# Layer 0 of a two-layer attention kernel: which maxima are turned at a unit's end, and where the totals of the unit before stand

## The chip, the cores and the metric

The kernel runs on one core of one Trainium2 chip. The metric is the device time of one execution in microseconds (us); less is better. Before the change it is 1690.28 us, the median of three runs (1688.93 to 1690.34).

## The reference, cut to what matters

Two attention layers over 1024 latent tokens and 256 context tokens of width 1024. The change touches the softmax attention of layer 0 alone: 16 heads of width 64, four heads share one key/value head. Latent queries see all 1280 keys, context queries only the 256 context keys.

```
def gqa_attend(q, k, v):
    s = jnp.einsum('bqhgd,bkhd->bhgqk', q, k).astype(jnp.float32) * (GQA_HEAD_DIM ** -0.5)
    p = jax.nn.softmax(s, axis=-1).astype(v.dtype)
    return jnp.einsum('bhgqk,bkhd->bqhgd', p, v)

def gqa_mixer(h, hc, p, cos, sin, with_ctx_out):
    ...
    o = sweep_query_blocks(lambda qb: gqa_attend(qb, k_all, v_all), q).reshape(B, S, GQA_WIDTH)
    y = (o * jax.nn.silu(g)) @ p["w_out"]
    ...
        oc = gqa_attend(qc, kc, vc).reshape(B, L, GQA_WIDTH)
        yc = (oc * jax.nn.silu(gc)) @ p["w_out"]
```

## The kernel before, in words

**Units.** Layer 0's attention runs over 20 units, one after the other, numbered here from 0. Sixteen are latent: one head, 1024 queries, ten tiles of 128 keys (`kts` has ten entries). Four are small, for the context queries of the four heads of a group: two key tiles. The small units stand at 4, 9, 18 and 19. The last latent unit, 17, is cut into a part of six key tiles and a part of four (`cut`).

**One unit, in stages.** For each key tile TensorE (PE) makes the scores (`st`, L545), transposed, so that keys lie on partitions and queries along the row. ScalarE (ACT) makes p = exp (L552). After the last tile comes the *unit's end*: PE multiplies the value tiles with all p (`avt`, L600, one pair of matmuls for the two halves of the queries, and since the operands are f32 each is two in the profile: four records per key tile).

**Maxima.** The softmax needs the largest score of each query beforehand. It is found ahead of time: between the score matmuls of one unit PE makes plain score products for later units into a PSUM tile `mx`, and VectorE (DVE) reduces each to a column of `m` (L430 for latent keys, L432 for context keys). One such step is issued for each key tile, 14 steps ahead at the start; a latent unit needs ten, a small one two. So the maxima of a small unit are done soon after those of the unit ahead of it, and all of them are done when unit 16 ends.

**A turn.** The maxima stand as columns and have to become rows. `do_shift` puts a function `turn` on the list `turns`: PE transposes `m` into an `mx` tile (L459), DVE copies the 8x128 result into the SBUF tile `crow` (L461), and two DMAs on SyncE's queue (SP) move it into one row of each half of the tile `shift` (L464). The scores of that unit take the row in as a fourth product (`st<-shift,minus`). `crow` has one buffer, and `mx` has two in PSUM. `run_turns` empties the whole list at each unit's end.

**Totals.** `finish` copies a unit's output out of PSUM and puts a function `total` on the list `totals`. It runs at the end of the next latent unit: PE sums p over partitions into an `mx` tile (L645, weights `twos`), DVE transposes and inverts it (L649, L650), a DMA spreads it (`rrow`, then `rb`), GpSimd (POOL) scales the output (L664, L665) and a DMA stores it in `od` (L669).

**Order at a unit's end.** PE, DVE and ACT take their instructions in the order of the code (`manual_schedule`); for SP and POOL a scheduler orders them. In `run` the end reads: turns, the pairwise sums of the last p tiles on DVE (`pair_sum`, L572), the totals of the unit before, a piece of weight loading for the output projection (`extra`, `parts`, at odd units; it splits f32 weights on ACT, L158, and on DVE or POOL, L137), then the value matmuls (`do_av`). When no maxima are left to compute, the output `avt` is not taken from the score tiles' pool but from the two `mx` buffers (`av_tile`); that is so from unit 16's end on.

Of the kernel before, what the change touches and what calls it, by code (L numbers as in the profile page):

```python
# [11 lines left out]
F32R = mybir.dt.float32r  # L12
# [7 lines left out]
P = 128  # L20
# [9 lines left out]
WIDE = (True, False)  # L30


def raw(ap):
    return ap.bitcast(F32)
# [3 lines left out]
def hybrid_kernel(ctx: ExitStack, tc: tile.TileContext, ins: dict, out: bass.AP):  # L38
# [197 lines left out]
    class Plan:  # L236
# [8 lines left out]
        def run(self):  # L245
            engines = mybir.EngineType
            with tc.manual_schedule(engines={engines.PE, engines.Activation, engines.DVE, engines.Pool, engines.SP}):
                for _, _, fn, args in sorted(self.todo, key=lambda e: e[:2]):
                    fn(*args)
# [60 lines left out]
    class Attention:  # L310
# [134 lines left out]
        def do_shift(self, u):  # L445

            s = self.state[id(u)]
            if u["kind"] == "lat":
                m = self.sm.tile([P, 8], F32, name="m1", tag="m1")
                dve.reduce_max(m, s["m"], axis=AX.X)  # L450
            else:
                m = s["m"][:, :, 0]

            def turn():
                if not WIDE[self.l]:
                    t = self.ps_m.tile([P, 512], F32, name="mx", tag="mx")[:8, :P]
                else:
                    t = self.ps_m.tile([P, 1024], F32, name="mx", tag="mx")[:8, :P]
                pe.transpose(t, m, ident)  # L459
                r = self.sm.tile([8, P], F32R, name="crow", tag="crow", bufs=1)  # L460
                dve.tensor_copy(r, t)  # L461
                if HALVES[self.l]:
                    for n in range(2):
                        sp.dma_start(raw(s["crow"][n]), raw(r[4 * n:4 * n + 4, :]))  # L464
                else:
                    sp.dma_start(raw(s["crow"]), raw(r))

            self.turns.append(turn)

        def start_unit(self):  # L470
            u = self.units[self.started]
# [115 lines left out]
                s["sum"] = t  # L587
            s["total"] = ([s["sum"]] if held else []) + last

        def do_av(self, u, group, ps):  # L590

            s = self.state[id(u)]
            kts = u["kts"]
            if group[0] == kts[0]:
                if not WIDE[self.l]:
                    s["av"] = self.ps_o.tile([P, 512], F32, name="av", tag="av")
                s["v"] = self.load_v(u)
            for kt, p in zip(group, ps):
                for n in range(2):
                    pe.matmul(s["av"][64 * n:64 * n + 64, :], lhsT=s["v"][:, kt, u["vc"]:u["vc"] + 64],  # L600
                              rhs=p[:, n * 512:(n + 1) * 512], start=kt == kts[0], stop=kt == kts[-1])
            if group[-1] == kts[-1]:
                self.finish(u)
# [66 lines left out]

            self.totals.append(total)

        def run_turns(self):
            while self.turns:
                self.turns.pop(0)()

        def run(self, lead, ahead, extra, tail):

            count = lead
            parts = None  # L680
            with tc.manual_schedule(engines={mybir.EngineType.PE, mybir.EngineType.DVE, mybir.EngineType.Activation}):
                for t, u in enumerate(self.units):
                    kts = u["kts"]
                    for v in self.units[t:t + 2]:
                        self.load_v(v)
                    while self.started < min(t + 1 + ahead, len(self.units)):
                        self.start_unit()
                    whole = len(kts) > 4
                    cut = 6 if u is self.last_lat else 0

                    def one_more():
                        nonlocal count
                        count += 1
                        self.maxima(count, t + 1 + ahead)

                    for group in (kts[:cut], kts[cut:]):
                        if not group:
                            continue
                        end = group[-1] == kts[-1]
                        final = t == len(self.units) - 1 and end  # L700
                        p2s = [self.pp.tile([P, 2, 1024], F32, name="p", tag="p", bufs=5) for _ in range(len(group) // 2)]
                        ps = [p2[:, a, :] for p2 in p2s for a in range(2)]

                        late = not whole and t >= len(self.units) - 2
                        n1 = len(ps) - (4 if whole and end else 2 if late else 0)
                        for i, kt in enumerate(group):
                            self.run_deferred(self.step)
                            if HALVES[self.l]:
                                count += 1 if WIDE[self.l] else 2
                                self.scores_by_halves(u, kt, ps[i], self.next_maxima(count, t + 1 + ahead))  # L710
                            else:
                                self.do_scores(u, kt, ps[i], one_more)
                            self.step += 1
                            if i < n1:
                                self.add_up(u, [ps[i]], [])
                        if end and t + 2 < self.started:
                            self.state[id(self.units[t + 2])].pop("rest", lambda: None)()
                        if final:
                            tail()
                        if WIDE[self.l] and group[0] == kts[0]:  # L720
                            self.av_tile(u)
                        self.run_turns()
                        if late or final:
                            self.add_up(u, [], ps[n1:])
                        elif n1 < len(ps):
                            sums = [self.pair_sum(p2) for p2 in p2s[n1 // 2:]]
                            self.add_up(u, *(([], sums) if cut else (sums, [])))
                        if final:
                            self.run_deferred(self.step + 2)
                        gap = 0  # L730
                        while self.totals and (whole or late or final):
                            self.totals.pop(0)(gap)
                            gap += 3
                        if t % 2 and end:
                            if parts:
                                parts()
                            parts = extra.pop(0)() if extra else None
                        self.do_av(u, group, ps)
                        self.step += (2 + len(group)) // 3
                gap = 0  # L740
                while self.totals:
                    self.totals.pop(0)(gap)
                    gap += 3
            self.run_deferred(self.step)
# [522 lines left out]
    def l0_open(at, st):  # L1267
        pool_ = st.enter_context(tc.tile_pool(name="shift0", bufs=1, **right))
        at.minus = pool_.tile([P, 4, P], F32R, name="minus")
        at.shift = pool_.tile([P, 512], F32R, name="shift")  # L1270
        pool.memset(raw(at.shift), 0.0)
        for i in range(4):
            a, b = (ident[:, j:j + 1].broadcast_to([P, P]) for j in (i, 64 + i))
            dve.scalar_tensor_tensor(at.minus[:, i, :], a, -1.0, b, op0=ALU.mult, op1=ALU.subtract)
# [89 lines left out]
    for g, pos in ((0, 4), (1, 9), (3, 18), (2, 19)):  # L1364
        units.insert(pos, ctxu[g])

    at = Attention(0, units, dict(scale=0.125, load=l0_load, scores=l0_scores, maxima=l0_maxima, mparts=1, open=l0_open, gaps=(4, 8, 11), kbufs=2, qbufs=3, vw=256))
    stE = ExitStack()
    with tc.tile_pool(name="wkg0a", bufs=4, **right) as wkg:
# [301 lines left out]
    for p_ in range(8):  # L1671
        for par in range(2):
            h = 2 * p_ + par
            units.append(dict(kind="lat", h=h, pair=p_, par=par, vg=(h // 4, 128 * (h // 2 % 2)), vc=64 * par,
                              kts=list(range(TT))))
    at = Attention(1, units, dict(scale=float(96 ** -0.5), load=l1_load, scores=l1_scores, maxima=l1_maxima, mparts=2, open=l1_open, gaps=(4, 6, 9),
                                  kbufs=3, qbufs=3, vw=128))
# [201 lines left out]
```

## Time and profile before

| what | value |
|---|---|
| median of three runs | 1690.28 us |
| the profiled execution's own time | 1689.1 us |
| its span, first to last instruction | 1687.3 us |
| PE busy | 1646.1 us, 98% of the span |
| DVE busy | 1044.1 us, 62% |
| POOL busy | 949.1 us, 56% |
| ACT busy | 641.2 us, 38% |
| unit 0's end begins (its transpose on PE) | 376.32 us |
| unit 16's end begins | 693.06 us |

Times in a profile's rows count from the first instruction. A row of the timeline has the start, the time to the last end, the engine, the line, the operation and its tiles, the shape, the number of merged instructions and, in brackets, how long the engine was idle before and what ended that. PEclk in a row by stretches is the granted TensorE clock, 1.00 at full speed. PE, busy 98%, is the engine whose idle time counts; for the others idle time counts where PE waits for them.

### The profile page before, as it was taken

Reading aid. Unit: us, or ns where it says so; the run is one execution under the profiler, and the core shown is the slowest. Engines: PE = TensorE matmul, PEld = TensorE weight load, DVE = VectorE, ACT = ScalarE, POOL = GpSimd, SP = SyncE. Lnnn points to the kernel's source line nnn. Section 1 sums busy time; section 2 is a strip of 40 time slices with the busy share of each in tenths; the row PEclk is TensorE's granted clock in tenths of the full one; section 3 lists DMA queues with packets and bytes.
Section 4 is the critical chain, followed back from the end, with each engine's and each line's share of the span. In section 5 each row is a group of like instructions: output and inputs, shape, how many; then the busy total and the mean of one; then the engine's idle time right before and its main releaser. Section 6 shows DMA issues by size and latency. Waiting matters only on the chain. (4 is left out here: it accounts for less than half of the span.)

```text
span 1687.3 us, 27273 instructions
## 1 busy us (share of the span) xinstructions
PE 1646.1 (98%) x10236; PEld 1191.6 (71%) x10236; DVE 1044.1 (62%) x1660; ACT 641.2 (38%) x944; POOL 949.1 (56%) x624
## 2 busy tenths in 40 slices
PE   8999999999999999899989999999999999999998
PEld 5776768875555555458878798886766767667587
DVE  3765553457787887426675657754777777777231
ACT  4642212235444555333234633330534434334310
POOL 2673431128889998742335644450668778777521
PEclk9999999999999999999999999999999999999999
DMA  9557855532342522256424866776565555653351
GB/s 311 176 147 236 268 155 180 160 94 57 99 116 76 138 70 70 55 148 195 141 80 131 238 176 187 227 206 150 126 143 139 132 131 120 134 135 82 121 172 70
DMA packets 221116, 244.21 MB, mean 145 GB/s; under 512 B 23160, under 2 KB 160616, under 8 KB 220984
## 3 DMA queue, kind: packets, MB, share of 16 engines
q1 hardware_dynamic: 220560, 242.36, 51.4%
q8 instruction: 81, 1.33, 0.3%
q14 instruction: 51, 0.42, 0.1%
q10 hardware_dynamic: 424, 0.11, 0.0%
HBM read 168.62 MB, written 73.63 MB: 144 GB/s over the span
## 5 line engine op out<-in xcount | busy, mean ns | idle before, releaser
L552 ACT ACTIVATE p<-st 128x1024 f32<-128x1024 f32 x328 | 336.2, 1027 | 154.1 <-PE st L545 140.8
L586 POOL TENSOR_TENSOR acp<-acp,p 128x1024 f32<-128x1024 f32 x128 | 305.1, 2384 | 7.8
L394 DVE TENSOR_REDUCE m<-mx 128x1 f32<-128x512 f32 x256 | 176.2, 691 | 93.7 <-PE mx L392 88.0
L430 DVE TENSOR_REDUCE m<-mx 128x1 f32<-128x1024 f32 x128 | 150.4, 1220 | 67.2 <-PE mx L421 66.7
L586 POOL TENSOR_TENSOR acp<-p 128x1024 f32<-128x1024 f32 x34 | 81.5, 2399 | 185.2 <-ACT p L552 185.2
L586 POOL TENSOR_TENSOR acp<-acp,acd 128x1024 f32<-128x1024 f32 x60 | 142.4, 2374 | 20.4 <-DVE acd L572 17.2
L600 PE MATMUL avt<-p,v 128*64 128x512 f32 x672 | 151.3, 602 | 1.6 <-DVE crow L461 1.5
L572 DVE TENSOR_REDUCE acd<-p 128x512 f32<-128x1024 f32 x124 | 144.7, 1220 | 7.8 <-ACT p L552 7.8
L600 PE MATMUL av<-p,v 128*64 128x512 f32 x640 | 141.1, 595 | 0.0
L137 POOL TENSOR_TENSOR wb<-wraw,wa 128x512 fp32r<-128x512 f32 (+3 forms) x65 | 85.9, 1337 | 81.8 <-ACT wa L158 80.9
L94 PE MATMUL mm<-wa,hh 128*128 128x512 f32 (+2 forms) x336 | 126.3, 376 | 1.7 <-ACT hh L947 1.7
L545 PE MATMUL st<-QH,KH 64*128 64x512 f32 x320 | 122.4, 407 | 0.6 <-DVE gth L304 0.5
L96 PE MATMUL mm<-wa,hl 128*128 128x512 f32 (+2 forms) x336 | 120.8, 360 | 1.4 <-DVE hl L950 1.4
L95 PE MATMUL mm<-wb,hh 128*128 128x512 f32 (+2 forms) x336 | 120.2, 358 | 0.0
L545 PE MATMUL st<-QH,KL 64*128 64x512 f32 x320 | 117.9, 391 | 0.0
L545 PE MATMUL st<-QL,KH 64*128 64x512 f32 x320 | 117.4, 390 | 0.0
L600 PEld LDWEIGHTS avt<-p,v 128*64 128x64 f32 x672 | 46.6, 138 | 96.6 <-issue 85.9
L94 PE MATMUL y<-wa,oh 128*128 128x512 f32 (+1 forms) x296 | 114.1, 386 | 0.6 <-ACT oh L786 0.6
L96 PE MATMUL y<-wa,ol 128*128 128x512 f32 (+1 forms) x296 | 113.5, 384 | 0.1
L95 PE MATMUL y<-wb,oh 128*128 128x512 f32 (+1 forms) x296 | 113.5, 383 | 0.0
L600 PEld LDWEIGHTS av<-p,v 128*64 128x64 f32 x640 | 44.4, 137 | 88.3 <-issue 87.6
L94 PE MATMUL mm<-hh,wa 128*128 128x512 f32 (+1 forms) x264 | 103.2, 391 | 0.2 <-DVE qt L1752 0.2
(247 smaller groups left out, 4031.3 us busy)
## 6 DMA issues: line engine op xcount, KB each, us to landing
mraw<-in_l_w_mod SPq DMA_DIRECT2D x64, 256.0 KB
wraw<-in_l_w_in SPq DMA_DIRECT2D x28, 512.0 KB
KH<-k1h SPq DMA_DIRECT2D x32, 320.0 KB
KL<-k1l SPq DMA_DIRECT2D x32, 320.0 KB
rb<-rrow SPq DMA_DIRECT2D x72, 128.0 KB
mraw<-in_l_w_mod SPq DMA_DIRECT2D x16, 512.0 KB
QA<-q0h SPq DMA_DIRECT2D x32, 256.0 KB
wraw<-in_l_w_out SPq DMA_DIRECT2D x16, 512.0 KB
```

Source lines behind the costliest of these rows:

```text
L94: pe.matmul(ps, lhsT=lh(k), rhs=rh(k), start=first and i == 0, stop=False)
L95: pe.matmul(ps, lhsT=lh(k), rhs=rl(k), start=False, stop=False)
L96: pe.matmul(ps, lhsT=ll(k), rhs=rh(k), start=False, stop=last and i == len(ks) - 1)
L137: eng.tensor_sub(lo, a, b)
L394: dve.reduce_max(s["m"][:, i, n:n + 1], held["m"], axis=AX.X)
L430: dve.reduce_max(s["m"][:, i, 0:1], m, axis=AX.X)
L545: pe.matmul(ps[:, n * 512:(n + 1) * 512], lhsT=lh, rhs=rh, start=j == 0, stop=j == last)
L552: act.activation(p, ps, AF.Exp, scale=self.ops["scale"])
L572: dve.reduce_sum(t[:, ns], p2.rearrange("p a n -> p n a")[:, ns, :], axis=AX.X)
L586: pool.tensor_add(t, a, b)
L600: pe.matmul(s["av"][64 * n:64 * n + 64, :], lhsT=s["v"][:, kt, u["vc"]:u["vc"] + 64], rhs=p[:, n * 512:(n + 1) * 512], start=kt == kts[0], ...
```

## The change

Only layer 0 (`WIDE`) is touched. Three things:

1. A unit's end t turns the maxima of unit t+1, and goes on over small units that follow directly (`next_turn`); turns of later units wait for a later end. So unit 4 is turned at the end of unit 3 and no longer of unit 2, unit 9 at the end of 8 and no longer of 7, and units 18 and 19 at the end of the first part of unit 17 and no longer at unit 16's.
2. The rows of maxima go through two buffers, `rows`, by the unit's number, and no longer through one `crow`.
3. At a latent unit's end the totals of the unit before are issued behind the first value tile (`postponed`), and so also behind the weight piece.

```
-                r = self.sm.tile([8, P], F32R, name="crow", tag="crow", bufs=1)
+                r = self.rows[self.units.index(u) % 2] if WIDE[self.l] else self.sm.tile([8, P], F32R, name="crow", tag="crow", bufs=1)
...
-            self.turns.append(turn)
+            self.turns.append((self.units.index(u), turn))
...
-        def do_av(self, u, group, ps):
+        def do_av(self, u, group, ps, second=None):
...
             for kt, p in zip(group, ps):
+                if second and kt == kts[1]:
+                    second()
...
-        def run_turns(self):
-            while self.turns:
-                self.turns.pop(0)()
+        def run_turns(self, upto=None):
+            while self.turns and (upto is None or self.turns[0][0] <= upto):
+                self.turns.pop(0)[1]()
...
+                    next_turn = t + 1
+                    while next_turn + 1 < len(self.units) and len(self.units[next_turn]["kts"]) <= 4:
+                        next_turn += 1
+                    if not WIDE[self.l]:
+                        next_turn = None
...
-                        self.run_turns()
+                        self.run_turns(next_turn)
...
-                        gap = 0
-                        while self.totals and (whole or late or final):
-                            self.totals.pop(0)(gap)
-                            gap += 3
+                        def sum_totals():
+                            gap = 0
+                            while self.totals and (whole or late or final):
+                                self.totals.pop(0)(gap)
+                                gap += 3
+
+                        postponed = WIDE[self.l] and whole and group[0] == kts[0]
+                        if not postponed:
+                            sum_totals()
                         if t % 2 and end:
                             if parts:
                                 parts()
                             parts = extra.pop(0)() if extra else None
-                        self.do_av(u, group, ps)
+                        self.do_av(u, group, ps, sum_totals if postponed else None)
...
+        at.rows = [pool_.tile([8, P], F32R, name=f"crow{i}") for i in range(2)]
```

On PE the end of unit 1, a plain one, before (numbers behind `m` only tell buffers apart; a count of 20 are the ten value tiles, two matmuls each):

```order
L545 MATMUL st<-shift,minus 128x512 x2
L459 MATMUL mx<-ident,m_3758 8x128
L645 MATMUL mx<-acp,twos 32x256 x4
L600 MATMUL avt<-p,v 64x512 x20
L421 MATMUL mx<-KA,QA 128x512 x2
```

and now, with line numbers 2 higher from the value matmuls on:

```order
L545 MATMUL st<-shift,minus 128x512 x2
L459 MATMUL mx<-ident,m_3758 8x128
L602 MATMUL avt<-p,v 64x512 x2
L647 MATMUL mx<-acp,twos 32x256 x4
L602 MATMUL avt<-p,v 64x512 x18
L421 MATMUL mx<-KA,QA 128x512 x2
```

The totals moved from ahead of the value matmuls to behind their first tile.

On PE the end of unit 16 before, where the maxima of units 17, 18 and 19 are turned:

```order
L545 MATMUL st<-shift,minus 128x512 x2
L459 MATMUL mx<-ident,m_6823 8x128
L459 MATMUL mx<-ident,m 8x128 x2
L645 MATMUL mx<-acp,twos 32x256 x4
L600 MATMUL avt<-p,v 64x512 x20
L545 MATMUL st<-QA,KA 128x512 x2
```

and now:

```order
L545 MATMUL st<-shift,minus 128x512 x2
L459 MATMUL mx<-ident,m_6808 8x128
L602 MATMUL avt<-p,v 64x512 x2
L647 MATMUL mx<-acp,twos 32x256 x4
L602 MATMUL avt<-p,v 64x512 x18
L545 MATMUL st<-QA,KA 128x512 x2
```

Two of three transposes are gone from here. They stand at the end of the first part of unit 17, on PE so far:

```order
L545 MATMUL st<-QL,KA 128x512 x2
L545 MATMUL st<-shift,minus 128x512 x2
L645 MATMUL mx<-acp,twos 32x256 x4
L600 MATMUL avt<-p,v 64x512 x12
L545 MATMUL st<-QA,KA 128x512 x2
```

and now:

```order
L545 MATMUL st<-shift,minus 128x512 x2
L459 MATMUL mx<-ident,m 8x128 x2
L602 MATMUL avt<-p,v 64x512 x2
L647 MATMUL mx<-acp,twos 32x256 x4
L602 MATMUL avt<-p,v 64x512 x10
L545 MATMUL st<-QA,KA 128x512 x2
```

On SP's queue, from unit 16's end on, before (`oraw` is the output projection's first fetch of `od`):

```order
L464 DMA shift<-crow 1x4x128 x6
L651 DMA rrow<-cr 128x8
L661 DMA rb<-rrow 64x512 x2
L659 DMA sg<-sgd_95 64x512
L669 DMA od_97<-os 64x512 x2
L659 DMA sg<-sgd_95 64x512
L755 DMA oraw<-od_97 128x7x128 x2
L651 DMA rrow<-cr 128x8
```

and now:

```order
L464 DMA shift<-crow_2950 1x4x128 x2
L653 DMA rrow<-cr 128x8
L663 DMA rb<-rrow 64x512 x2
L661 DMA sg<-sgd_95 64x512
L671 DMA od_97<-os 64x512 x2
L661 DMA sg<-sgd_95 64x512
L767 DMA oraw<-od_97 128x7x128 x2
L464 DMA shift<-crow_2949 1x4x128 x2
L464 DMA shift<-crow_2950 1x4x128 x2
L653 DMA rrow<-cr 128x8
```

The four row DMAs of units 18 and 19 stand behind one store of `od` and two fetches from it.

## The prediction

> **What bounds the kernel now.** I read the page's busy line first: PE is the bound. Then the waits of PE alone, over layer 0's attention (375 to 712 us).
>
> ```profile
> PE 1646.1 (98%) x10236; PEld 1191.6 (71%) x10236; DVE 1044.1 (62%) x1660; ACT 641.2 (38%) x944; POOL 949.1 (56%) x624
> PE mx L645 <- DVE m L430: 3.4, 11, 0.4
> PE mx L645 <- DVE crow L461: 2.6, 1, 2.6
> PE avt L600 <- DVE crow L461: 1.5, 1, 1.5
> PE mx L459 <- DVE m L430: 0.4, 2, 0.2
> PE mx L459 <- DVE m L432: 0.2, 1, 0.2
> ```
>
> PE's whole idle time here is 8.1 us, all at units' ends, all on DVE, in two kinds: short waits of the totals (L645) for an `mx` buffer that a reduction still reads, and two long ones behind a copy to `crow`. No other engine stands in PE's way, so a microsecond taken off a unit's end is a microsecond of the span. Next, the timeline of PE at four ends: unit 0 (no totals yet), unit 1 (plain), unit 2 (turns units 3 and 4) and unit 3.
>
> ```profile
> 376.32 0.27 PE L459 MATMUL mx<-ident,m 128*8 128x128 f32 x1
> 376.53 8.80 PE L600 MATMUL avt<-p,v 128*64 128x512 f32 x40
> 385.26 0.50 PE L421 MATMUL mx<-KA,QA 64*128 64x512 f32 x2
> ...
> 396.74 0.39 PE L545 MATMUL st<-QL,KA 64*128 64x512 f32 x2
> 396.96 0.40 PE L545 MATMUL st<-shift,minus 64*128 64x512 f32 x2
> 397.29 0.27 PE L459 MATMUL mx<-ident,m 128*8 128x128 f32 x1
> 397.85 0.64 PE L645 MATMUL mx<-acp,twos 128*32 128x256 f32 x8 [0.28 <-DVE m L430]
> 398.41 8.80 PE L600 MATMUL avt<-p,v 128*64 128x512 f32 x40
> 407.15 0.49 PE L421 MATMUL mx<-KA,QA 64*128 64x512 f32 x2
> ...
> 419.20 0.27 PE L459 MATMUL mx<-ident,m 128*8 128x128 f32 x1
> 419.65 0.27 PE L459 MATMUL mx<-ident,m 128*8 128x128 f32 x1 [0.18 <-DVE m L430]
> 429.24 0.50 PE L421 MATMUL mx<-KA,QA 64*128 64x512 f32 x2
> ...
> 441.29 0.27 PE L459 MATMUL mx<-ident,m 128*8 128x128 f32 x1
> 441.95 0.64 PE L645 MATMUL mx<-acp,twos 128*32 128x256 f32 x8 [0.39 <-DVE m L430]
> 451.25 0.51 PE L421 MATMUL mx<-KA,QA 64*128 64x512 f32 x2
> ```
>
> Read starts, since matmuls overlap. An end, from first transpose to the next unit's first product, takes 8.94 us without totals, 9.86 in unit 1, 10.04 in unit 2, 9.96 in unit 3. Steps of unit 1: transpose to totals 0.56, totals to value tiles 0.56, value tiles 8.74. In unit 0 the value tiles follow 0.21 behind the transpose.
>
> Unit 16's end, on PE, on DVE, and by stretches (PEclk is the first of the last three figures):
>
> ```profile
> 693.06 0.27 PE L459 MATMUL mx<-ident,m 128*8 128x128 f32 x1
> 693.55 0.46 PE L459 MATMUL mx<-ident,m 128*8 128x128 f32 x2 [0.21 <-DVE m L432]
> 696.58 1.08 PE L645 MATMUL mx<-acp,twos 128*32 128x256 f32 x8 [2.58 <-DVE crow L461]
> 699.14 10.89 PE L600 MATMUL avt<-p,v 128*64 128x512 f32 x40 [1.48 <-DVE crow L461]
> 709.96 0.50 PE L545 MATMUL st<-QA,KA 64*128 64x512 f32 x2
> ...
> 693.41 0.27 DVE L461 CAST crow<-mx 8x128 fp32r<-8x128 f32 x1
> 696.16 0.28 DVE L461 CAST crow<-mx 8x128 fp32r<-8x128 f32 x1 [2.48 <-DMA shift<-crow]
> 698.80 0.28 DVE L461 CAST crow<-mx 8x128 fp32r<-8x128 f32 x1 [2.37 <-DMA shift<-crow]
> ...
> 671.10:681.00 9.90, 9.62 (x51) 3.05 (x49) 5.84 (x8) 1.12 (x2) 9.24 (x4) 1.00 0.35 100
> 696.50:703.40 6.90, 5.34 (x18) 1.48 (x20) 4.59 (x5) 0.00 (x0) 2.68 (x2) 0.51 0.01 1
> ```
>
> This end takes 16.90 us. Three turns go through one `crow`: the second and the third copy wait 2.5 us each for the DMA that still reads it. Totals and `avt` share the two `mx` buffers with the turns, so PE waits 2.58 and 1.48 us behind these copies. On top of it the granted clock is halved for 6.9 us: the value tiles take 10.82 us (699.14 to 709.96) in place of 8.74, so 2.1 us are lost to the clock alone.
>
> **The change, part by part.** Signs: plus is gained.
>
> *A plain end* (1, 5, 6 and 10 to 15: nine ends; 5 and 10 sum two units, which changes nothing here). The value tile follows 0.21 behind the transpose, the totals wait for nothing, since the buffer's reduction ends about 0.4 behind the transpose (totals started at +0.56) and a value tile lasts 0.87 (8.73 / 10). The totals' own 0.56 remain. New is one more change of matmul shape: leaving the value tiles and coming back. Leaving a shape costs 0.10, by scores to transpose (396.96 to 397.29, 0.33) against scores to scores (396.74 to 396.96, 0.22). Coming back to value tiles is in no row alone; between 0 and another 0.10 I take the middle, 0.05. So 0.21 + 8.74 + 0.56 + 0.15 = 9.66 against 9.86: +0.20. Nine times: +1.8.
>
> A rule speaks against this move: the Trainium skill, TensorEngine Tiling (Array Packing), Key Properties, says that changing the tiling mode drains the engine. The 0.33 against 0.22 above agrees in direction. By the rule the sum is as I take it or less; if a change of shape cost nothing, the sum below would be 2.3 us larger (fifteen ends by 0.15).
>
> *Ends 2 and 7* lose their second transpose as well: 10.04 to 9.66, +0.38, twice +0.8.
>
> *Ends 3 and 8* now turn two units. The second transpose needs the buffer that the totals wait for now, so it comes some 0.60 behind the first (the totals start at +0.66 there, and 419.65 shows a transpose 0.45 behind): 0.60 + 0.21 + 8.74 + 0.56 + 0.15 = 10.26 against 9.96: −0.3, twice −0.6. With two `rows` the copies no longer wait for a DMA.
>
> *End 16* keeps one turn. Its `avt` stands in an `mx` buffer, so the first value tile waits for the last reduction as the second transpose does now (693.55, +0.49) instead of starting at +0.21: 9.94 against 16.90, +6.96. In this are the two long waits (4.06), the halved clock (2.1 in the value tiles, some 0.2 in the totals) and the two transposes.
>
> *Unit 17's first part* receives the two turns.
>
> ```profile
> 716.48 0.39 PE L545 MATMUL st<-shift,minus 64*128 64x512 f32 x2
> 716.79 0.64 PE L645 MATMUL mx<-acp,twos 128*32 128x256 f32 x8
> 717.36 5.37 PE L600 MATMUL avt<-p,v 128*64 128x512 f32 x24
> ...
> 699.73 0.57 SPq L464 DMA_DIRECT2D shift<-crow  x1
> 704.29 0.32 SPq L651 DMA_DIRECT2D rrow<-cr  x1
> 714.79 0.98 SPq L755 DMA_DIRECT2D oraw<-od  x2
> ```
>
> All maxima are done by then, so both transposes run at once; `avt` shares the first one's buffer and waits for its copy: 0.33 to the transpose, about 0.35 to the copy (693.06 to 693.41), 0.27 for it and some 0.04 to PE, 0.99 in all against 0.31 to the totals now. With the 0.15 of the split: −0.83.
>
> *DMAs.* Four row DMAs (0.6 us of queue each) move on SP behind the two `oraw` fetches, which wait for a store of unit 15. Now that fetch ends 5.8 us into unit 17 (715.77 less 709.96). The chain to it starts with unit 15's inverse on DVE, just ahead of 704.29; without the copies' waits it comes 5.4 us sooner (698.80 less 693.41), and unit 17 starts 7.0 sooner, so the fetch ends about 7.4 into the unit. Its transposes come at 6.85 and the copies are done by 7.7, so SP is just free. Four issues take 2.5; the landing is bounded by 693.41 to 696.16, in which a copy, two issues and the landing lie, so about 1.2 behind the last issue. The rows are there at 11.4. The second part needs them with its fourth product: 6.85, then 0.66 to the first value tile, 0.56 and 0.15 for the totals, 5.3 for six tiles (717.36, 5.37 long, its last record overlapping what follows) and 0.8 for three products: 14.3. Cover: 2.9 us. Elsewhere rows have nearly the whole end of 9.7 us.
>
> *The weight piece* at odd ends now stands ahead of the totals' inverse on DVE. Its subtraction delays inverse, `rrow` and the release of the `mx` buffer; DVE has the time:
>
> ```profile
> 447.13 1.19 DVE L137 TENSOR_TENSOR wb<-wraw,wa 128x512 fp32r<-128x512 f32 x1
> 451.80 1.23 DVE L430 TENSOR_REDUCE m<-mx 128x1 f32<-128x1024 f32 x1 [3.48 <-PE mx L421]
> ```
>
> 3.48 us idle behind it, cost nil; were the cover gone, the next unit's first maximum would wait by what is over. On POOL two `os` products swap places with a first addition, hidden in the same way.
>
> *Sum:* 1.8 + 0.8 − 0.6 + 6.96 − 0.83 = 8.1 us. The profiled execution took 1689.1 (span 1687.3): 1681.0. The median of the runs shown, 1690.28, lies 1.2 above it: **1682.2 us**, 0.48% less. What follows layer 0 starts earlier by as much; PE's waits there name DVE, ACT and POOL alone, no transfer that would keep its own time.
>
> **The rivals.**
>
> *A dearer split* (0.11). If leaving and re-entering the value tiles costs 0.5 instead of 0.15, fifteen splits take 5.3 us more: gain 2.8, 1687.5, no change that can be told. For it: every split adds two changes of shape between dense matmuls. Against: 716.48 to 716.79 and 376.32 to 376.53 show changes at 0.1 over the pitch. Near the other end, at no cost, stands 1680.
>
> *The slow clock stays* (0.08). The gain is then 8.1 − 2.3 = 5.8: 1684.5. Rows speak against it: the clock is 1.00 in the plain end before, and 0.51 from the end of the 2.58-us wait on.
> The Trainium skill (TensorE: Matmul & The Clock Gate, Part 1) has the clock halve after at least one idle window of about 3.4 us; read as one unbroken wait of that length, it would not put this stretch down to these waits, and by it the time is this rival's. The trace has it halved after 2.58 us of waiting.
>
> *Late rows, slower* (0.05). If the store that the `oraw` fetches wait for landed later, the four row DMAs would come late and PE would stand in unit 17's second part. It decides from 2.9 us of lateness; with a halved clock after it (2.3) it takes 2.9 + 8.1 − 2.3, nearly 9 us late, to be slower than before, say 12 late: 1693. Against: POOL and DVE wait on nothing new in that chain.
>
> **How the numbers follow.** The forecast holds 0.76, the rivals 0.11, 0.08 and 0.05. Its own bounds: with splits free 1680; a second stretch of half clock, elsewhere, may come or go:
>
> ```profile
> 884.20:887.80 3.60, 3.44 (x12) 2.56 (x12) 1.87 (x9) 1.18 (x6) 2.33 (x9) 0.53 0.35 112
> ```
>
> It is worth 1.7 us (half of 3.4). Below that I go to 1679; above, the slow clock (1684.5) and part of the dearer split: 1687. No change means within 0.2%, 3.4 us, about what this measurement can tell. Faster by more: forecast and slow clock, 0.84; same 0.11; slower 0.05.
>
> **What would show it.** Right: no wait on the copies to `crow` in DVE's or PE's list; plain ends of 9.66 and a unit 16's end near 9.9 with PEclk 1.00; ends 3 and 8 near 10.3; the totals (L645 before, L647 after) wait at no plain end. Wrong: value tiles that restart late behind the totals; a wait of the scores for `shift` in unit 17; totals that wait for something other than the reduction.

## The result, and the profile after

The kernel after takes 1683.24 us, the median of nine runs (1680.52 to 1686.67); the kernel before took 1689.37 us in the same comparison. The ratio is 0.9962 (0.9953 to 0.9971), so 4.9 to 7.9 us are gained. Timed a second time (experiment 8 below) the ratio is 0.9954 (0.9939 to 0.9970): 1680.91 beside 1689.73 us. The forecast of 1682.2 us lies between the two medians. The first profiled execution of after took 1686.67 us, the slowest of its nine. One execution of a kernel changed for an experiment (experiment 4) took 8036.65 us, and the ratios leave it out.

The waits of PE in the profile after, over the same 375 to 712 us as in the prediction (line, waited for, engine and line behind it, us in all, times, longest):

```profile
PE mx L421 <- DVE m L430: 1.2, 1, 1.2
PE mx L459 <- DVE m L430: 0.6, 2, 0.3
PE st L545 <- ACT p L552: 0.6, 2, 0.3
PE avt L602 <- DVE m L432: 0.2, 1, 0.2
```

The eleven waits of the totals and the two long ones behind `crow` are gone. New is one wait of 1.2 us of a score product for the maxima (L421); it does not stand at an end that the change touches, and it is the one thing that the forecast did not have.

PE's timeline after, at the ends of unit 1 (plain) and unit 3 (turns units 4 and 5):

```profile
400.14 0.27 PE L459 MATMUL mx<-ident,m 128*8 128x128 f32 x1
400.34 1.08 PE L602 MATMUL avt<-p,v 128*64 128x512 f32 x4
401.35 0.64 PE L647 MATMUL mx<-acp,twos 128*32 128x256 f32 x8
401.92 7.95 PE L602 MATMUL avt<-p,v 128*64 128x512 f32 x36
409.80 0.50 PE L421 MATMUL mx<-KA,QA 64*128 64x512 f32 x2
...
443.51 0.27 PE L459 MATMUL mx<-ident,m 128*8 128x128 f32 x1
444.08 0.27 PE L459 MATMUL mx<-ident,m 128*8 128x128 f32 x1 [0.30 <-DVE m L430]
...
453.74 0.50 PE L421 MATMUL mx<-KA,QA 64*128 64x512 f32 x2
```

Read starts again. Unit 1's end takes 9.66 us (409.80 less 400.14): 0.20 to the first value tile, 1.01 for that tile, 0.57 for the totals, 7.88 for nine tiles. The totals wait for nothing. Unit 3's end takes 10.23, with 0.57 from transpose to transpose.

Unit 16's end and the end of unit 17's first part on PE, a stretch of unit 16's end (PEclk is the first of the last three figures), and SP's queue:

```profile
695.24 0.27 PE L459 MATMUL mx<-ident,m 128*8 128x128 f32 x1
695.73 1.08 PE L602 MATMUL avt<-p,v 128*64 128x512 f32 x4 [0.21 <-DVE m L432]
696.74 0.64 PE L647 MATMUL mx<-acp,twos 128*32 128x256 f32 x8
705.18 0.50 PE L545 MATMUL st<-QA,KA 64*128 64x512 f32 x2
...
712.00 0.38 PE L459 MATMUL mx<-ident,m 128*8 128x128 f32 x2
712.65 1.08 PE L602 MATMUL avt<-p,v 128*64 128x512 f32 x4 [0.26 <-DVE crow L461]
718.67 0.50 PE L545 MATMUL st<-QA,KA 64*128 64x512 f32 x2
...
694.50:704.50 10.00, 9.79 (x55) 3.28 (x53) 6.54 (x9) 1.81 (x2) 9.53 (x5) 1.00 0.05 13
...
711.54 0.99 SPq L767 DMA_DIRECT2D oraw<-od  x2
712.63 2.67 SPq L464 DMA_DIRECT2D shift<-crow  x4
```

Unit 16's end takes 9.94 us (16.90 before), at full clock. Unit 17's first part ends 6.67 us behind its first transpose. The second `oraw` fetch leaves SP at 712.53, the four row DMAs follow at once, and no score waits for a row.

From unit 0's end to the first product of the output projection, the stretch that the change touches and that I call *the attention* from here on, the profile before has 366.22 us and the profile after 359.43: 6.8 less. By ends:

| end of unit | before | after | forecast |
|---|---|---|---|
| 1, 6, 11 to 15 | 9.85 to 9.87 | 9.66 | 9.66 |
| 5, 10 (two totals) | 10.30, 10.32 | 10.09 | 0.20 less |
| 2, 7 | 10.04 | 9.66 | 9.66 |
| 3, 8 | 9.96, 9.97 | 10.23, 10.25 | 10.26 |
| 16 | 16.90 | 9.94 | 9.94 |
| 17, first part with its scores | 12.70 | 13.49 | 0.83 more |
| scores of units 9 and 10, with unit 9's value tiles | 16.66 | 18.16 | no change |

The ends alone give 8.2 us. The last row takes 1.5 back. Its place in the profile after, on DVE, POOL and PE (unit 9's value tiles are done on PE at 551.20, unit 10's scores follow):

```profile
551.19 2.62 DVE L137 TENSOR_TENSOR wb<-wraw,wa 128x512 fp32r<-128x512 f32 x1 [1.79 <-ACT wa L158]
553.74 4.61 DVE L430 TENSOR_REDUCE m<-mx 128x1 f32<-128x1024 f32 x4
...
550.87 2.40 POOL L586 TENSOR_TENSOR acp<-p 128x1024 f32<-128x1024 f32 x1
...
555.01 0.50 PE L421 MATMUL mx<-KA,QA 64*128 64x512 f32 x2 [1.24 <-DVE m L430]
```

and in the profile before, on DVE and POOL:

```profile
549.23 0.69 DVE L137 TENSOR_TENSOR wb<-wraw,wa 128x512 fp32r<-128x512 f32 x1 [1.76 <-ACT wa L158]
...
547.90 1.27 POOL L664 TENSOR_TENSOR rb<-rb,sg 128x512 f32<-128x512 f32 x1
549.25 1.83 POOL L665 TENSOR_TENSOR os<-os,rb 128x512 f32<-128x512 f32 x1
```

The same subtraction of a weight piece on DVE takes 0.69 us in one and 2.62 in the other. Where it is long, POOL's first addition started 0.32 ahead of it; the reductions behind it come late, both `mx` buffers stay full, and PE stands 1.24 us. Whether the change does this was the question that the experiments had to settle. There are two theories: A, the changed order puts POOL ahead of DVE there; B, it is chance, in either kernel.

### The profile page after: what moved, and what is told of

Read it like the earlier page. It is cut to its first block, busy times and chain, and to the rows that moved or that the text cites. A ratio compares the mean times of both kernels' runs of the same rounds, so it can differ in the third digit from the quotient of the medians.

```text
span 1684.9 us, 27275 instructions
## 1 busy us (share of the span) xinstructions
PE 1648.9 (98%) x10236; PEld 1194.2 (71%) x10236; DVE 1046.5 (62%) x1660; ACT 640.7 (38%) x944; POOL 950.6 (56%) x624
## 5 line engine op out<-in xcount | busy, mean ns | idle before, releaser
L430 DVE TENSOR_REDUCE m<-mx 128x1 f32<-128x1024 f32 x128 | 150.4, 1220 | 68.9 <-PE mx L421 68.4
```

Of the source, the lines that this page charges most:

```text
L430: dve.reduce_max(s["m"][:, i, 0:1], m, axis=AX.X)
```

## The experiments

**1. Turns and buffers without the later totals** (from after).

```
-                        postponed = WIDE[self.l] and whole and group[0] == kts[0]
+                        postponed = False
```

> The change without its third part: turns and two row buffers as changed, totals back ahead of the value tiles. Theory (the turns at the end of unit 16 carry the gain; POOL, no longer held back at unit 7's end, then runs against DVE's weight subtraction at unit 9's end): ends 2 and 7 gain 0.18 each, ends 3 and 8 lose 0.2 each, unit 16's end 7.0, unit 17's first part -0.7, in all 6.3, less about 1.4 for a wait of PE behind DVE in unit 10: about 4.9 us, 1684.5. No stretch of halved clock at unit 16's end. Rival (the split of the value tiles carries the gain): next to nothing, over 1688. Rival (the wait in unit 10 is chance): 6.3 us and no such wait.

Measured: 1683.55 us, ratio 0.9961 (0.9948 to 0.9975). The attention takes 361.43 us, 4.8 less than before and 2.0 more than after. Plain ends stay at 9.86, ends 2 and 7 lose 0.18, unit 16's end is 9.88. The subtraction at unit 9's end takes 2.30 us, and PE waits 0.9 us there. So nearly all of unit 16's gain needs no later totals, and the new wait can come without them.

**2. The later totals alone** (from after: all turns at the earliest end, one buffer).

```
-                r = self.rows[self.units.index(u) % 2] if WIDE[self.l] ...
+                r = self.rows[0] if WIDE[self.l] ...
-                        self.run_turns(next_turn)
+                        self.run_turns()
```

> The third part alone: totals behind the first value tile, all turns at the old ends, through one row buffer. Theory: nine plain ends gain 0.20, ends 3 and 8 0.3, ends 2 and 7 lose 0.07, unit 16's end keeps two DMA waits and the halved clock, now in one PE wait of some 5 us, and loses up to 1: gain 0.8 to 1.8, about 1688. No wait in unit 10, since DVE still waits at unit 7's end and POOL stays as late as before. Rival (the split carries the gain): 4 us or more. Rival (the wait in unit 10 comes from the moved totals): it shows here.

Measured: 1687.8 us, ratio 0.9982 (0.9973 to 0.9991); the attention 364.54, 1.7 less than before. Plain ends are 9.66, ends 2 and 7 10.12, unit 16's end 17.33. Unit 16's end on PE, and a stretch of it:

```profile
693.91 1.08 PE L602 MATMUL avt<-p,v 128*64 128x512 f32 x4 [2.50 <-DVE crow L461]
696.65 1.08 PE L647 MATMUL mx<-acp,twos 128*32 128x256 f32 x8 [1.66 <-DVE crow L461]
...
695.50:702.40 6.90, 5.75 (x20) 1.71 (x22) 5.41 (x7) 0.00 (x0) 3.39 (x2) 0.51 0.01 2
```

With one buffer the two waits stay, at other instructions and not joined into one of some 5 us as expected, and the halved clock stays with them. PE does not wait in unit 10: the subtraction at unit 9's end takes 1.34 us.

**3. Three buffers alone** (from before).

```
-                r = self.sm.tile([8, P], F32R, name="crow", tag="crow", bufs=1)
+                r = self.rows[self.units.index(u) % 3] if WIDE[self.l] and self.units.index(u) % 3 < 2 else self.sm.tile([8, P], F32R, name="crow", tag="crow", bufs=1)
...
+        at.rows = [pool_.tile([8, P], F32R, name=f"crow{i}") for i in range(2)]
```

> The kernel before with three row buffers in turn, nothing else moved: three turns still stand at unit 16's end, but no copy waits for a DMA. Theory (the single row buffer is what makes PE wait, not the number of turns): unit 16's end falls from 16.9 to about 10.5, clock 1.00 throughout, other ends as before, gain 6.4, less 1.4 for the wait in unit 10: 5.0, about 1684.4. Rival (the two shared mx buffers make PE wait): unit 16's end stays near 16, no gain.

Measured: 1685.33 us, ratio 0.9964 (0.9951 to 0.9977); the attention 360.94, 5.3 less than before, with 0.6 us of the wait at unit 10 in it. Unit 16's end on PE, with all three turns still in it:

```profile
695.29 0.27 PE L459 MATMUL mx<-ident,m 128*8 128x128 f32 x1
695.76 0.46 PE L459 MATMUL mx<-ident,m 128*8 128x128 f32 x2 [0.20 <-DVE m L432]
696.50 0.64 PE L645 MATMUL mx<-acp,twos 128*32 128x256 f32 x8 [0.28 <-DVE crow L461]
697.07 8.80 PE L600 MATMUL avt<-p,v 128*64 128x512 f32 x40
705.80 0.50 PE L545 MATMUL st<-QA,KA 64*128 64x512 f32 x2
```

The end takes 10.51 us in place of 16.90: the value tiles are back at 8.73. Buffers without any moved turn bring 6.4 of the 6.96 us of this end. Moving the two turns brings another 0.6 there and costs 0.8 in unit 17, so with three buffers it gains nothing by itself; with two it keeps the copies from waiting for each other's row.

**4. The waits filled, the buffer kept** (from before): at unit 16's end PE makes 18 pairs of score products that nothing uses, 11 behind the transposes and 7 behind the totals.

```
+                        fill = WIDE[self.l] and t == 16
+                        def keep_busy(k):
+                            ...
+                            for _ in range(k):
+                                for n in range(2):
+                                    pe.matmul(ft[:, n * 512:(n + 1) * 512], lhsT=prods[n][0], rhs=prods[n][1], start=True, stop=True)
+                        if fill:
+                            keep_busy(11)
...
+                        if fill:
+                            keep_busy(7)
```

> The kernel before with 18 pairs of unused score products on PE at unit 16's end, 11 behind the three transposes and 7 behind the totals, as long as PE's two waits there (2.58 and 1.48 us). Their results are read by nothing. Theory (the halved clock follows from these waits): PEclk stays 1.00, the value tiles take 8.74 us again and the totals 0.56, unit 16's end falls from 16.9 to about 14.6 though PE does more; 2.3 us gained. Rival (the clock halves there for another reason): the end stays at 16.9 and the stretch at half clock too.

Measured on PE and by a stretch as long as the halved one before:

```profile
694.68 0.27 PE L459 MATMUL mx<-ident,m 128*8 128x128 f32 x1
698.25 0.64 PE L645 MATMUL mx<-acp,twos 128*32 128x256 f32 x8
700.76 8.80 PE L600 MATMUL avt<-p,v 128*64 128x512 f32 x40
709.49 0.51 PE L545 MATMUL st<-QA,KA 64*128 64x512 f32 x2
...
696.50:703.40 6.90, 6.86 (x52) 3.48 (x52) 3.25 (x5) 0.00 (x0) 2.56 (x2) 1.00 0.02 4
```

The end takes 14.8 us in place of 16.9, at full clock, though the value tiles start 6.08 us behind the first transpose in both (700.76 less 694.68, 699.14 less 693.06). So the halved clock is a consequence of PE's standing still, and was worth 2.1 us (2.3 were expected). The kernel as a whole did not gain: 1693.08 us, ratio 1.0012 (0.9998 to 1.0027). One profile shows why in part: the subtraction at unit 9's end took 2.36 us (PE waits 1.0), and the parts behind the attention took 949.2 us against 944.8 before, of which 3.4 are a stretch of half clock near 1144 us that no other profile has. Why that one came is not settled. The attention itself takes 365.63 us, 2.2 less than in the profile of before that has the long subtraction too (367.83, experiment 7).

Theory A had here its first point against it: this kernel has the old order up to unit 16, with DVE's wait for `crow` at unit 7's end, and the long subtraction all the same.

**5. The subtraction at unit 9's end moved to POOL** (from after).

```
-                                parts()
+                                parts() if whole else parts(0)
```

> The changed kernel with the one weight subtraction that DVE does at unit 9's end given to POOL. Theory (DVE's subtraction, 2.6 us in place of 0.7 beside POOL's first addition, delays two reductions and PE waits 1.24 us for their mx buffer in unit 10): that wait is gone, 1.4 us faster than the changed kernel, 1681.5 or so. Rival (any delay at that place costs the same, since POOL is nearly full there): the wait moves to POOL's sums or the totals, no gain.

Measured: 1682.24 us, ratio 0.9951 (0.9936 to 0.9966). The attention takes 358.00 us, 8.2 less than before; the scores of units 9 and 10 take 16.73, and PE waits for L430 at the two second transposes alone; no new wait came up at POOL's sums or at the totals. The timing does not tell this kernel from the changed one (ratios 0.9962 and 0.9954). What one profile without the wait is worth, experiment 7 shows.

**6. One turn more ahead** (from after: at unit 7's end units 8 and 9 are turned through one buffer, as in before).

```
+                    if t == 7:
+                        next_turn = 9
...
-                r = self.rows[self.units.index(u) % 2] if WIDE[self.l] ...
+                r = self.rows[0 if self.units.index(u) == 9 else self.units.index(u) % 2] if WIDE[self.l] ...
```

> The changed kernel with one DMA wait put back: units 8 and 9 are both turned at unit 7's end, through one row buffer, so DVE stands there some 2.7 us for the DMA as before; the weight subtraction at unit 9's end is on DVE as in the changed kernel. Theory (that wait kept POOL late and so out of the way of the subtraction): unit 7's end +0.45, unit 8's -0.57, and the wait of PE in unit 10 (1.24) is gone, attention 357.9 in place of 359.4. Rival (the wait in unit 10 has nothing to do with unit 7's end): it stays, 359.3.

Measured: 1680.76 us, ratio 0.9942 (0.9926 to 0.9958); the attention 357.88, no wait at unit 10, the subtraction 0.71 us. Taken by itself this speaks for theory A. The next four profiles show that it can't be read so.

**7. The same kernels profiled again**, two more executions each of before and after, nothing edited.

> The kernel before, unchanged, profiled once more. Question: is the 1.2 us wait of unit 10's scores, which the kernel after shows, set by the order of the work or by chance? Theory A (order: the wait of DVE for the third row's transfer at unit 7's end keeps POOL late, so DVE's weight subtraction at unit 9's end starts ahead of POOL's first addition): score stage of units 9 and 10 at 16.7 us, the subtraction at 0.7 us. Theory B (chance: POOL's time there hangs on when unit 7's and unit 8's rows land, which moves by 1 us from one execution to the next): the subtraction is short where POOL's first addition starts behind it and 2 to 2.6 us where it started ahead, in either kernel; the stage is 16.7 or 17.6 to 18.2 us. In both theories the subtraction ends about 0.55 us behind the POOL operation in whose time it started.

> The kernel before, a third profile. Theory A: stage of units 9 and 10 at 16.7 us again. Theory B: with the busy-work kernel, which keeps the old order up to there and showed the long subtraction, one or more of the four profiles of the old order have it long.

> The kernel after, unchanged, profiled once more. Theory A: the subtraction at unit 9's end long (2 to 2.6 us), scores of unit 10 wait 0.9 to 1.3 us, stage 17.6 to 18.2 us. Theory B: long or short, by whether POOL's first addition starts ahead of it. Attention of layer 0 359.4 us where long, 358.0 where short.

> The kernel after, a third profile: as for the second. Without DVE's wait at unit 7's end POOL is ahead in every profile by theory A; by theory B not in every one.

The kernel before, second profile, on DVE and POOL, and PE's wait of it:

```profile
550.72 2.61 DVE L137 TENSOR_TENSOR wb<-wraw,wa 128x512 fp32r<-128x512 f32 x1 [1.76 <-ACT wa L158]
...
550.39 2.39 POOL L586 TENSOR_TENSOR acp<-p 128x1024 f32<-128x1024 f32 x1
...
PE mx L421 <- DVE m L430: 1.2, 1, 1.2
```

The kernel after, third profile, on DVE and POOL:

```profile
547.19 0.69 DVE L137 TENSOR_TENSOR wb<-wraw,wa 128x512 fp32r<-128x512 f32 x1 [1.79 <-ACT wa L158]
...
546.01 1.29 POOL L667 TENSOR_TENSOR os<-os,rb 128x512 f32<-128x512 f32 x1
547.25 2.88 POOL L586 TENSOR_TENSOR acp<-p 128x1024 f32<-128x1024 f32 x1
```

Before has the long subtraction, after the short one: theory A falls, B stands. The three profiles of each kernel at that place (POOL's operation is the one that runs when the subtraction starts; lead is how much earlier it started):

| profile | POOL's operation, lead, its end | subtraction, its end | scores of 9 and 10 | attention |
|---|---|---|---|---|
| before | none | 0.69, 549.92 | 16.66 | 366.22 |
| before, second | addition, 0.33, 552.78 | 2.61, 553.33 | 18.14 | 367.83 |
| before, third | product L665, 0.23, 550.44 | 1.61, 550.99 | 17.13 | 367.89 |
| after | addition, 0.32, 553.27 | 2.62, 553.81 | 18.16 | 359.43 |
| after, second | addition, 0.51, 550.60 | 2.43, 551.15 | 17.95 | 359.26 |
| after, third | product L667, 1.18, 547.30 | 0.69, 547.88 | 16.72 | 358.03 |

In every row with an operation of POOL the subtraction ends 0.54 to 0.58 us behind that operation, and so it does in experiments 1, 2, 3, 4 and 6: its length is the time that POOL's operation still needs, and some 0.55 us more. Like beside like, short beside short the attention falls by 8.2 us (366.22 to 358.03), long beside long by 8.4 (367.83 to 359.43). The third profile of before is long for another reason: its halved clock began 5.2 us behind unit 16's first transpose in place of 3.4, so that nearly all of it fell on the value tiles, and unit 16's end took 17.76 us in place of 16.90.

Whether the change makes the long subtraction more frequent, these profiles can't tell. It took over 2 us in two of four with the old order (before and experiment 4), and in three of four of after (the fourth is in experiment 8).

What moves POOL shows one step back. In the four profiles with the old order POOL's product of unit 7 waits for its row's transfer (before, its third and its second profile, experiment 4):

```profile
528.49 1.29 POOL L664 TENSOR_TENSOR rb<-rb,sg 128x512 f32<-128x512 f32 x1 [3.01 <-DMA rb<-rrow]
...
528.36 1.30 POOL L664 TENSOR_TENSOR rb<-rb,sg 128x512 f32<-128x512 f32 x1 [3.75 <-DMA rb<-rrow]
...
528.35 1.30 POOL L664 TENSOR_TENSOR rb<-rb,sg 128x512 f32<-128x512 f32 x1 [2.09 <-DMA rb<-rrow]
...
526.71 1.30 POOL L664 TENSOR_TENSOR rb<-rb,sg 128x512 f32<-128x512 f32 x1 [1.95 <-DMA rb<-rrow]
```

It starts 20.7 us ahead of the subtraction where that takes 0.69 us, 21.0 where it takes 1.61, and 22.4 and 22.6 where it takes 2.61 and 2.36. In the first two SP issues `rb` 3.3 us behind `rrow`, in the others 1.4, with nothing else on its queue between. POOL is busy almost without a gap from there on, so the time at which one small transfer lands is carried to unit 9's end, where 0.3 us decide. In the four profiles of after it is unit 8's product that waits for its row: it starts 2.9, 3.1 and 3.2 us ahead of the long subtractions and 2.5 ahead of the short one. What moves the transfer is open.

**8. The kernel after, timed again.**

> The kernel after, unchanged, timed once more beside the kernel before, five rounds. The first comparison gave 6.1 us less (ratio 0.9962, 0.9953 to 0.9971), the steps of the forecast 8.1 us, and layer 0's attention in three profiles of each kernel differs by 8.4 us on the mean. If the 2 us between are a real cost outside of layer 0's attention, the ratio comes out at 0.996 again. If they are the chance of the first runs (parts that the change does not touch took 1327 us there against 1320 to 1323 in five other profiles, and the clash at unit 9's end comes and goes in both kernels), it comes out near 0.995, 1682 us beside 1690.3.

Measured: 1680.91 us beside 1689.73, ratio 0.9954 (0.9939 to 0.9970), 5.1 to 10.3 us less; in its profile the attention takes 358.98 us (subtraction 2.29). The forecast's 8.1 us lie in this interval, and 0.2 us outside the first one. Own time less attention is 1327.2 us in the first profile of after and 1320.5 to 1321.9 in the three others; a part of the surplus is in the granted clock. Stretches of the first profile of after, and of the third:

```profile
29.10:32.50 3.40, 3.40 (x12) 2.72 (x11) 1.94 (x4) 1.63 (x3) 2.51 (x2) 0.50 1.06 361
879.00:885.80 6.80, 5.84 (x17) 4.38 (x18) 3.14 (x13) 2.78 (x10) 3.42 (x11) 0.50 0.38 105
...
876.20:879.60 3.40, 3.40 (x12) 2.33 (x11) 1.60 (x7) 2.18 (x9) 1.81 (x6) 0.51 0.23 74
```

The third has no halved stretch near 29 us, and near 876 one of half the length. Each of the two differences is worth up to 1.7 us, and neither lies in layer 0's attention. So the 2 us by which the first comparison falls short of the forecast are not a cost that the change brings every time; what made them in the nine executions, of which one was profiled, is not shown.

**9. Both small costs taken out** (experiment 5, and the second turn of ends 3 and 8 behind the first value tile).

```
-                        self.run_turns(next_turn)
+                        self.run_turns(next_turn, 1 if t in (3, 8) and WIDE[self.l] else 99)
...
                         def sum_totals():
+                            if WIDE[self.l] and t in (3, 8):
+                                self.run_turns(next_turn)
```

> The changed kernel with the weight subtraction of unit 9's end on POOL, and at ends 3 and 8 the second turn behind the first value tile, ahead of the totals. Theory: the second transpose no longer waits for the last reduction, ends 3 and 8 fall from 10.23 to about 9.87; 0.7 us less than with the subtraction alone, layer 0's attention from unit 0's end 357.3 us in place of 358.0. Rival (the copy, now behind the pairwise sums on DVE, brings the row too late): PE waits for shift at the start of units 4 and 9.

Measured: 1680.71 us, ratio 0.9946 (0.9928 to 0.9963); the attention 357.20, the shortest of all. Unit 3's end on PE:

```profile
440.69 0.27 PE L459 MATMUL mx<-ident,m 128*8 128x128 f32 x1
440.89 1.08 PE L602 MATMUL avt<-p,v 128*64 128x512 f32 x4
441.90 0.27 PE L459 MATMUL mx<-ident,m 128*8 128x128 f32 x1
...
450.55 0.50 PE L421 MATMUL mx<-KA,QA 64*128 64x512 f32 x2
```

The end takes 9.86 us in place of 10.23: the second transpose no longer waits, and no score waits for `shift`. By the profile this version is 0.8 us better than after at its best; the timing cannot tell them apart.

## Why the prediction was right, point by point

*The plain ends.* 9.66 was forecast and measured. The split's price came out as forecast, 0.15, but otherwise divided: a value tile lasts 0.87, the first one takes 1.01 until the totals start (0.14 for leaving), nine tiles take 7.88 (0.02 for coming back). So the dearer split does not happen. Without the later totals the 0.20 are missing (experiment 1, 9.86), and the later totals alone bring them (experiment 2, 9.66). The Trainium skill (TensorEngine Tiling (Array Packing), Key Properties) says that a change of tiling mode drains the engine. The trace agrees in direction, with the 0.14 and 0.02 us above.

*Ends 2, 7, 3 and 8*: 9.66, 9.66, 10.23 and 10.25, within 0.03 of the forecast (9.66 and 10.26). The second transpose at ends 3 and 8 waits for a reduction (L430), as the prediction had it.

*End 16*: 9.94 as forecast. Two of its three parts are shown apart: the two waits go with buffers alone (experiment 3), and the halved clock goes with the waits (it stays in experiment 2, where they stay, and is gone in experiment 4, where they are filled). The clock was worth 2.1 us, 2.3 in the forecast. The two transposes are the third part, some 0.6 us (10.51 in experiment 3, 9.88 in experiment 1). So the rival with the slow clock fell for its reason. The Trainium skill (TensorE: Matmul & The Clock Gate, Part 1) has the clock halve after at least one idle window of about 3.4 us. Read as one unbroken wait, that is not what these traces show: the clock was halved with waits of 2.58 and 1.48 us before and of 2.50 and 1.66 us in experiment 2.

*Unit 17* cost 0.79 (0.83 forecast). The `oraw` fetch ended 7.35 us into the unit (7.4 forecast), the rows followed at once, and no score waited for them: the late rows did not happen.

*The weight piece* was costed at nil from a row at unit 3's end, where DVE idles 3.48 us behind it. As a statement on the change that held, since unit 9's end, a small unit's, keeps its order. As a reading of the kernel it was too wide: behind unit 9's subtraction there is no idle time (551.19 for 2.62 us, then 553.74), and PE's 1.2 us hang on it. What the prediction lacked is that the base moves: the sum was taken from one execution, and that one had the short subtraction, the best of three. The profile before could have warned. The same subtraction took 0.69 us at this end and 1.19 at unit 3's, where it ended 0.56 us behind POOL's additions (438.01 to 447.76, and 447.13 for 1.19). The range had room for it, but for other causes; that the first comparison with its 6.1 us stayed inside is in that respect luck.

## What to carry to other kernels

A buffer that a transfer still reads stalls whoever writes it next. Where the engine that bounds the kernel waits behind that, look at its granted clock as well, because the wait can cost more than its own length (here 4.06 us of waiting and 2.1 us of halved clock). One buffer for each write in flight gives back both (three in experiment 3, two where the turns stand apart). Before a new wait is put down to a change, profile the same kernel again: an instruction whose time depends on what another engine does at that moment can show a wait in one execution and none in the next. Such an instruction can be put on the engine with which it collides, if that one has the time: in experiment 5 the wait is gone, though the time of the whole kernel is too coarse to show it.

## What the runs showed of the hardware

A subtraction of two f32 tiles of 128x512 in SBUF takes 0.69 us on DVE, and up to 2.62 us if an addition or product on POOL is under way. It does not run slower at an even rate, it waits: in eleven profiles, over leads of 0.23 to 1.18 us, it ended 0.54 to 0.58 us behind POOL's operation, whose own time stayed at 2.38 to 2.40 us (additions) or 1.27 to 1.29 (products). The other way round POOL waits: the operation behind a short subtraction took 1.83 us in place of 1.27 in the first profile of before, and 2.88 in place of 2.39 in the third of after. The Trainium skill (SBUF — State Buffer, Who interferes with whom) says that a DVE instruction with two SBUF inputs and a GpSimd instruction that reads SBUF exclude each other, and that the one that starts first keeps the other out for its whole length; these traces agree.

The granted clock falls by half for 3.4 or 6.8 us at a time, in each of the fourteen profiles, so one stretch more or less moves an execution by up to 1.7 or 3.4 us, of the size of the effects told apart here. At unit 16's end PE was not idle throughout before the clock fell: in the 3.4 us ahead of it PE was busy 0.69, 0.88 and 0.64 us in the three profiles of before, and 1.08 in experiment 2. In experiment 4, where the clock stayed at 1.00, PE was busy 3.20 us of the first 3.4 from the first transpose on. What share in between suffices, no run here shows.
